# Two products of an encoder kernel by Strassen's algorithm for three of eight row pairs, with its sums on VectorE and in accumulating DMAs

## The chip, the cores and the metric

The kernel runs on one core of a Trainium2 chip. Its engines work beside one another, each through its own list of instructions in order: TensorE (PE, the matmuls, with their weight loads shown as PEld), VectorE (DVE), ScalarE (ACT), GpSimd (POOL), SyncE (SP, which here only issues DMAs), and the DMA engines. They wait for one another on semaphores. The metric is the device time of one launch in microseconds; the median of three runs before is 2689.91 us (2688.54 to 2690.1).

## What is computed

Two layers of an encoder over 256 tokens of width 2048, in float32, and a final norm:

```python
for l in range(DEPTH):                       # DEPTH = 2
    u = rmsnorm(x, norm_mix[l])
    proj = u @ w_in[l]
    ...                                      # latent attention y_a, neighbourhood attention y_b
    merged = jax.nn.sigmoid(gate_a) * y_a + jax.nn.sigmoid(gate_b) * y_b
    x = x + merged @ w_out[l]                # 2048 x 2048

    h = rmsnorm(x, norm_mlp[l]) @ w_ff1[l]   # 2048 x 8192
    x = x + jnp.square(jax.nn.relu(h)) @ w_ff2[l]   # 8192 x 2048

return rmsnorm(x, norm_final)
```

## The kernel before

x stays on the chip as two tiles `xt` of 128 tokens by 2048. All products run in a float32 made of two parts: an operand is split into `hi`, its value rounded to the matmul's type, and `lo`, the rest, and a product is the sum of three matmuls, hi x hi, hi x lo and lo x hi. An activation is kept transposed, 128 of its features by 256 tokens, as a tile `pair` whose left half is `hi` and right half `lo`. A weight is loaded once, as a 1 MB tile `raw` (L167, issued by SP, three buffers), cast to `hi` by ACT (L172) and subtracted to `lo` by DVE (L173), in pieces of 1024 columns with four buffers each (HBUFS).

There are two forms of product. `gemm_a` (L215) gives 128 tokens by 512 features: two PSUM banks, one for each half of the tokens, three matmuls of 512 columns for each 128 x 512 block of weight and half of the tokens (L199 to L201). `gemm_b` (L227) gives features by tokens: the weight is the stationary operand, and one matmul of 512 columns (both parts of the activation) and one of 256 (L194, L195) do a block. Of the eight PSUM banks five are for these products (`bank`) and three for attention, transposes and norms (`abank`).

A layer runs: w_in in pieces, with attention between them, gates and the two output projections, which merge into `part[t, c4]` (L597 to L600); w_out as four `gemm_a` of 512 features, whose sums are added to x by DVE (`residual`, L612, L617); then the MLP in four blocks of 2048 hidden features: `gemm_b` for w_ff1 (four calls of 512 features), squared ReLU (`relu2`, L639), `gemm_a` for w_ff2 (four calls), whose sums are multiplied by the squared norm scale and added to x by DVE (L619). The MLP's norm is thus applied after both products, as one factor for each token. In the last block, and after w_out, the squares of the new x are summed by ACT (L296) for the next norm, and the new x is transposed by PE (`turned_x`, L326) and split (L150, L154).

Engines get their instructions in the order in which a scheduler places them, and each executes its own in that order. Small work is written as generators that wait in `pending`: `tick`, called between the matmuls of a product, advances one that is due; `drain` runs all. So the transposes of the merged `part` for w_out stand between the matmuls of the next gate, those of x between the matmuls of the next product, and the norm's row (`rows_of`, L242, matmul L250) some 100 matmuls into the product after it.

## Time and profile before

| | |
|---|---|
| median of three runs | 2689.91 us |
| profiled execution: its time, its span | 2689.91 us, 2688.1 us |
| matmuls of `gemm_a` and attention's values, L199 to L201 | 3 x 2240 |
| matmuls of `gemm_b`, L194 and L195 | 2 x 3008 |
| weights loaded, with all other transfers | 496.49 MB, mean 185 GB/s |

The rows of the profile are read so. A group is the line of the program, the engine, the operation, the tile written and the tiles read, the sizes, the count; then the busy time of all in us, the mean of one in ns; then the idle time of the engine just ahead of them and what ended it. A row of a timeline is the start and length in us. The record of a matmul reaches past its slot, so the pace is read from the starts. In a row of a window the columns are the stretch, then for PE, PEld, DVE, ACT and POOL the busy us and the count, then PE's granted clock, the busy share of the DMA engines and GB/s. A wait is given as the waiting engine and line, what it waited for, the us in all, the times, the longest. A DMA group gives the queue, the count, the KB of each and the median us from issue to landing.

### The profile page before, as it was taken

To read this page: it belongs to the slowest core of one execution; us is meant where nothing else is said; L and a number is where in the kernel's file an instruction comes from. 1 tells how busy PE (TensorE), PEld (TensorE's weight loads), DVE (VectorE), ACT (ScalarE), POOL (GpSimd) and SP (SyncE) were. 2 spreads that over 40 slices of the span, in tenths; PEclk is the share of its full clock that TensorE was granted. 3 is DMA by queue.
4 is the path that set the end of the run, shared out by engine and by line. 5 is a ranking of instruction groups with operands and counts; after the bars stand their busy time and mean duration, and the time that the engine had idled before them with its cause. 6 is when DMAs were issued, how large, how long until landed. Compare 5 with 4: busy or idle time off the path is not lost.

```text
span 2688.1 us, 34037 instructions
## 1 busy us (share of the span) xinstructions
PE 2666.8 (99%) x13596; PEld 2268.7 (84%) x13596; DVE 1602.9 (60%) x2158; ACT 1277.1 (48%) x1815; POOL 60.5 (2%) x86
## 2 busy tenths in 40 slices
PE   8999999999999999999999999999999999999998
PEld 7888888888888888888888888888888888888886
DVE  5676486555655546556567754955556555565554
ACT  5554465444434434444445544644444344443443
POOL 1110000000000000000001100000000000000000
PEclk9999999999999999999999999999999999999999
DMA  7555644555565555555555555455555555655554
GB/s 231 184 165 189 195 161 155 189 184 180 186 203 186 190 190 186 197 193 189 183 183 179 171 187 183 153 167 188 188 188 188 189 187 194 208 189 193 188 188 141
DMA packets 253839, 496.49 MB, mean 185 GB/s; under 512 B 12688, under 2 KB 16784, under 8 KB 253680
## 3 DMA queue, kind: packets, MB, share of 16 engines
q1 hardware_dynamic: 250624, 488.14, 55.2%
q0 software_dynamic: 2048, 4.56, 0.6%
q8 instruction: 106, 1.74, 0.3%
q10 hardware_dynamic: 1008, 1.61, 0.2%
q14 instruction: 53, 0.43, 0.0%
HBM read 492.18 MB, written 2.10 MB: 184 GB/s over the span
## 4 chain that ended last, share of the span: by engine, by line
PE 84%; issue 14%; DVE 1%; DMA 1%; ACT 0%; POOL 0%; SPq 0%; POOLq 0%; DVEq 0%; ACTq 0%
PE bank L194 21%; PE bank L199 16%; PE bank L200 16%; PE bank L201 16%; PE bank L195 11%; DMA raw<-in_w_in 1%; PE abank L206 1%; PE abank L205 1%; PE abank L204 1%; PE abank L326 1%; PE abank L377 0%; DVE lo L173 0%; DVE wide L670 0%; PE abank L347 0%; ACT hi L172 0%
## 5 line engine op out<-in xcount | busy, mean ns | idle before, releaser
L173 DVE TENSOR_TENSOR lo<-raw,hi 128x1024 fp32r<-128x1024 f32 (+1 forms) x928 | 1132.5, 1222 | 977.8 <-ACT hi L172 973.0
L172 ACT CAST hi<-raw 128x1024 fp32r<-128x1024 f32 (+1 forms) x928 | 971.8, 1049 | 1131.1 <-PE bank L201 736.2
L194 PE MATMUL bank<-pair,hi 128*128 128x512 f32 x3008 | 1059.0, 398 | 2.3 <-DVE small L212 1.0
L200 PE MATMUL bank<-lo,pair 128*128 128x512 f32 (+1 forms) x2240 | 866.1, 387 | 0.0
L199 PE MATMUL bank<-hi,pair 128*128 128x512 f32 (+1 forms) x2240 | 865.8, 388 | 0.0
L201 PE MATMUL bank<-hi,pair 128*128 128x512 f32 (+1 forms) x2240 | 865.8, 387 | 0.0
L195 PE MATMUL bank<-pair,lo 128*128 128x256 f32 x3008 | 835.5, 280 | 0.4 <-DVE lo L173 0.3
L194 PEld LDWEIGHTS bank<-pair,hi 128*128 128x128 f32 x3008 | 563.5, 188 | 133.0 <-ACT hi L172 1.9
L195 PEld LDWEIGHTS bank<-pair,lo 128*128 128x128 f32 x3008 | 567.7, 189 | 5.9 <-DVE lo L173 1.6
L201 PEld LDWEIGHTS bank<-hi,pair 128*128 128x128 f32 x2240 | 420.8, 188 | 84.6
L199 PEld LDWEIGHTS bank<-hi,pair 128*128 128x128 f32 x2240 | 420.8, 188 | 84.1
L200 PEld LDWEIGHTS bank<-lo,pair 128*128 128x128 f32 x2240 | 420.9, 188 | 82.6
L150 ACT ACTIVATE pair<-small 128x256 fp32r<-128x256 f32 x200 | 73.6, 413 | 89.8 <-DVE small L641 67.1
L210 ACT COPY small<-bank 128x256 f32<-128x256 f32 x218 | 78.6, 369 | 29.0 <-PE bank L195 27.8
L152 DVE TENSOR_TENSOR pair<-small,pair 128x256 fp32r<-128x256 f32 x200 | 76.6, 418 | 19.2 <-ACT pair L150 19.2
L212 DVE TENSOR_TENSOR small<-bank,small 128x256 f32<-128x256 f32 x218 | 83.0, 416 | 0.2
L259 POOL TENSOR_TENSOR col<-var,mhalf 128x2 f32<-128x2 f32 x9 | 6.3, 702 | 1928.8 <-DVE var L257 1928.8
L619 DVE SCALAR_TENSOR_TENSOR xt<-bank,sq,xt 128x512 f32<-128x512 f32 x64 | 45.0, 744 | 7.8 <-PE bank L201 7.8
L641 DVE SCALAR_TENSOR_TENSOR small<-small 128x256 f32<-128x256 f32 x128 | 48.2, 418 | 0.0
L154 DVE SCALAR_TENSOR_TENSOR pair<-abank,g_sb,pair 128x256 fp32r<-128x256 f32 x64 | 29.2, 478 | 23.0 <-ACT pair L150 23.0
L150 ACT ACTIVATE pair<-abank,g_sb 128x256 fp32r<-128x256 f32 x64 | 28.2, 469 | 27.3 <-PE abank L326 23.4
L150 ACT ACTIVATE pair<-abank 128x256 fp32r<-128x256 f32 x64 | 23.6, 381 | 29.2 <-PE abank L206 19.1
(96 smaller groups left out, 789.9 us busy)
## 6 DMA issues: line engine op xcount, KB each, us to landing
raw<-in_w_ff SPq DMA_DIRECT2D x256, 1024.0 KB, 5.0
raw<-in_w_in SPq DMA_DIRECT2D x124, 1024.0 KB, 5.1
raw<-in_w_out SPq DMA_DIRECT2D x32, 1024.0 KB, 4.9
raw<-in_w_o_na SPq DMA_DIRECT2D x16, 1024.0 KB, 4.9
raw<-in_w_o_mla SPq DMA_DIRECT2D x16, 1024.0 KB, 4.9
raw<-in_w_ukv SPq DMA_DIRECT2D x8, 1024.0 KB, 4.9
raw<-in_w_uq SPq DMA_DIRECT2D x8, 768.0 KB, 4.6
raw<-in_w_in SPq DMA_DIRECT2D x10, 512.0 KB, 4.9
```

Source lines behind the costliest of these rows:

```text
L150: nc.scalar.activation(dst[:, :S], src, AF.Copy, scale=scale)
L152: nc.vector.tensor_tensor(dst[:, S:], src, dst[:, :S].bitcast(F32), op=ALU.subtract)
L172: nc.scalar.copy(hi, src)
L173: nc.vector.tensor_tensor(lo, src, hi.bitcast(F32), op=ALU.subtract)
L194: nc.tensor.matmul(ps, wh, a, start=first, stop=False)
L195: nc.tensor.matmul(ps[:, :S], wl, a[:, :S], start=False, stop=last)
L199: nc.tensor.matmul(ps, a[:, t * P:(t + 1) * P], wh, start=first, stop=False)
L200: nc.tensor.matmul(ps, a[:, t * P:(t + 1) * P], wl, start=False, stop=False)
L201: nc.tensor.matmul(ps, a[:, S + t * P:S + (t + 1) * P], wh, start=False, stop=last)
L210: nc.scalar.copy(h, ps[:, S:])
L212: nc.vector.tensor_tensor(t, ps[:, :S], h, op=ALU.add)
L641: nc.vector.scalar_tensor_tensor(t, t, 0.0, t, op0=ALU.max, op1=ALU.mult)
```

## The change

w_out and w_ff2 go to a new product, `gemm_s` (L360). It takes 256 rows of weight (a row pair j, eight in 2048 rows) by 1024 features as a 2 x 2 matrix of 128 x 512 blocks, and the activations for them as a 2 x 2 matrix of 128 features by 128 tokens. Five pairs are multiplied as before, 8 products of three matmuls each. The pairs in `SPAIRS`, 2, 4 and 6, are multiplied by Winograd's form of Strassen's algorithm, 7 products of three matmuls, for which four sums of weight blocks (`t`, L405 to L408) and four of activation blocks (`operand`, L333 to L336) are formed on DVE. All eight PSUM banks are in use: seven for the products, an eighth for the block that the ordinary pairs add to directly. One call covers 1024 features, so w_out is two calls (g = 0, 1), and w_ff2 two for each block. At its end `evac` adds the products up: a copy on ACT (L741), three sums on DVE (L742, L744, L746), then into x four products straight from PSUM on DVE (L748, L750 to L753) and four sums by `put`: on DVE (L735) in w_out and the last block, where squares of x follow, by accumulating DMAs from GpSimd (L733) in the first three blocks of each layer.

With it go other edits. `hi` and `lo` are 2048 columns wide in the second half of a layer, three buffers each; the pools of the two halves are opened and closed apart (`half_a`, `half_b`), and `drain` runs at the end of each. The transposes of `part` (`turned_pair`, L347) are started only after that drain, at the start of w_out. The MLP's norm is applied to the hidden features, as a row in `relu2` (L786), whose squares move to ACT (L787), so that the sums into x need no factor. The squares' sum of a Norm moves from GpSimd to DVE. The layer ends with a drain, which puts the next norm's row ahead of w_in's matmuls. The loads of the final gain move to the last block. One tag of eight PSUM banks takes the place of five and three.

```diff
-NSLOT, ABANKS, SMALL, RBUFS, HBUFS = 44, 3, 8, 3, 4
+NSLOT, SMALL, RBUFS, HBUFS = 44, 8, 3, 4
+SPAIRS = (2, 4, 6)
...
+            if hbufs == 3:
+                if k0 % 4 == 0:
+                    his = wpool.tile([P, 2048], F32R, tag="hi", name="hi", bufs=hbufs)
+                    los = wpool.tile([P, 2048], F32R, tag="lo", name="lo", bufs=hbufs)
...
-            nc.gpsimd.tensor_tensor(self.acc, self.acc, sq, op=ALU.add)
+            nc.vector.tensor_tensor(self.acc, self.acc, sq, op=ALU.add)
...
+    def operand(f, strassen):
+        a11, a21, a12, a22, s1, s2, s3, s4 = (f[:, i] for i in range(8))
+        if strassen:
+            nc.vector.tensor_tensor(s1, a21, a22, op=ALU.add)
+            nc.vector.tensor_tensor(s2, s1, a11, op=ALU.subtract)
+            nc.vector.tensor_tensor(s4, a12, s2, op=ALU.subtract)
+            nc.vector.tensor_tensor(s3, a21, a11, op=ALU.subtract)
+        hi, lo = [], []
+        for i in range(0, 8 if strassen else 4, 4):
+            src = f[:, i:i + 4].rearrange("p a q -> p (a q)")
+            h, lw = pair(), pair()
+            nc.scalar.copy(h, src)
+            nc.vector.tensor_tensor(lw, src, h.bitcast(F32), op=ALU.subtract)
...
+    def gemm_s(w, c0, acts, evac):
...
+        for j in range(n):
...
+            if j not in SPAIRS:
+                ws = parts(raw)
+                for k in range(2):
+                    left, right = ws[2 * k:2 * k + 2]
+                    ah, al = have(acts, j)
+                    for i, t, side in ((2, 0, right), (3, 0, left), (4, 1, right), (8, 1, left)):
+                        mm3(i, ah[2 * k + t], al[2 * k + t], *side)
...
+            b12, b11, b22, b21 = (raw[:, i:i + 512] for i in range(0, 2048, 512))
+            ts = wpool.tile([P, 4, 512], F32, tag="t", name="t", bufs=2)
+            t1, t3, t2, t4 = (ts[:, i] for i in range(4))
+            nc.vector.tensor_tensor(ts[:, :2], b12.rearrange("p (a n) -> p a n", a=1).to_broadcast([P, 2, 512]),
+                                    raw[:, 512:1536].rearrange("p (a n) -> p a n", a=2), op=ALU.subtract)
+            nc.vector.tensor_tensor(t2, b22, t1, op=ALU.subtract)
+            nc.vector.tensor_tensor(t4, b21, t2, op=ALU.subtract)
+            w11, w22, w21 = parts(raw[:, 512:])
+            w1, w3, w2, w4 = parts(ts.rearrange("p a n -> p (a n)"))
...
+            mm3(1, a11, l11, *w11)
+            mm3(2, a12, l12, *w21)
+            mm3(3, s4, r4, *w22)
+            mm3(5, s1, r1, *w1)
+            mm3(7, s3, r3, *w3)
+            mm3(6, s2, r2, *w2)
+            mm3(4, a22, l22, *w4)
+        evac(b)
...
-                if t == 1:
-                    start(turned(lambda t, c4=c4: part[t, c4], c4, mg, lambda c: 0.5), 2)
...
+        drain()
+        half_a.close()
...
+            def put(x, u):
+                if n is None:
+                    nc.gpsimd.dma_start(x, u, accum_op=ALU.add)
+                else:
+                    nc.vector.tensor_tensor(x, x, u, op=ALU.add)
...
+                nc.scalar.copy(p1, b[1])
+                nc.vector.tensor_tensor(u2, p1, b[6], op=ALU.add)
+                put(x11, p1)
+                nc.vector.tensor_tensor(u4, u2, b[5], op=ALU.add)
+                put(x12, u4)
+                nc.vector.tensor_tensor(u3, u2, b[7], op=ALU.add)
+                put(x21, u3)
+                nc.vector.tensor_tensor(x22, x22, b[5], op=ALU.add)
+                put(x22, u3)
+                nc.vector.tensor_tensor(x12, x12, b[3], op=ALU.add)
+                nc.vector.tensor_tensor(x11, x11, b[2], op=ALU.add)
+                nc.vector.tensor_tensor(x22, x22, b[8], op=ALU.add)
+                nc.vector.tensor_tensor(x21, x21, b[4], op=ALU.add)
...
-                nc.vector.scalar_tensor_tensor(t, t, 0.0, t, op0=ALU.max, op1=ALU.mult)
+                nc.vector.scalar_tensor_tensor(t, t, 0.0, mlp.row, op0=ALU.max, op1=ALU.mult)
+                nc.scalar.activation(relu2.f[:, 2 * (m % 2):2 * (m % 2) + 2].rearrange("p a q -> p (a q)"), t, AF.Square)
...
         if not last:
             start(norm.scales(), 10)
+            while pending:
+                drain()
+        half_b.close()
```

ACT at the first start of w_out, before: `th` is the gate's tanh, `hi` a weight, `pair` from `abank` the transposed and scaled `part`.

```order
L533 ACTIVATE th<-bank,half 128x512 x2
L172 CAST hi<-raw 128x1024 x7
L150 ACTIVATE pair<-abank 128x256 x3
L172 CAST hi<-raw 128x1024
L150 ACTIVATE pair<-abank 128x256
L172 CAST hi<-raw 128x1024 x5
```

The same place in the changed program; `f` is the transposed `part`, L382 the weights of `gemm_s`.

```order
L643 ACTIVATE th<-bank,half 128x512 x2
L189 CAST hi<-raw 128x1024
L355 ACTIVATE f<-bank 128x512
L341 CAST pair<-f 128x512
L382 CAST hi<-raw 128x2048 x2
L355 ACTIVATE f<-bank 128x512
L341 CAST pair<-f 128x512
L355 ACTIVATE f<-bank 128x512
L382 CAST hi<-raw 128x1536
```

Before, casts of weights went on between the copies of the transposed tiles, with several casts ahead of each; now the first copy and its cast stand ahead of the first weight of w_out.

DVE in the first block of w_ff2 before, where one call follows another: `lo` is a weight's rest, `xt_91` and `xt_92` the two tiles of x.

```order
L173 TENSOR_TENSOR lo<-raw,hi 128x1024 x7
L619 SCALAR_TENSOR_TENSOR xt_91<-bank,sq,xt_91 128x512
L619 SCALAR_TENSOR_TENSOR xt_92<-bank,sq,xt_92 128x512
L173 TENSOR_TENSOR lo<-raw,hi 128x1024 x8
L619 SCALAR_TENSOR_TENSOR xt_91<-bank,sq,xt_91 128x512
```

The same in the changed program, where its second call follows the first: `wide` is a sum of the evacuation, `xt_88` and `xt_89` are x, `t` the sums of weights.

```order
L742 TENSOR_TENSOR wide<-wide,bank 128x512
L383 TENSOR_TENSOR lo<-raw,hi 128x2048
L744 TENSOR_TENSOR wide<-wide,bank 128x512
L746 TENSOR_TENSOR wide<-wide,bank 128x512
L748 TENSOR_TENSOR xt_89<-xt_89,bank 128x512
L383 TENSOR_TENSOR lo<-raw,hi 128x2048
L751 TENSOR_TENSOR xt_88<-xt_88,bank 128x512
L405 TENSOR_TENSOR t<-raw 128x1024
L383 TENSOR_TENSOR lo<-raw,hi 128x1536
L750 TENSOR_TENSOR xt_88<-xt_88,bank 128x512
L753 TENSOR_TENSOR xt_89<-xt_89,bank 128x512
L407 TENSOR_TENSOR t<-raw,t 128x512
```

Two updates of x between runs of equal `lo` have become eight steps that stand between the next call's `lo` and its sums of weights.

PE where the second layer begins, before: L194 and L195 are w_in's matmuls, L250 the norm's row.

```order
L194 MATMUL bank<-pair,hi 128x512
L195 MATMUL bank<-pair,lo 128x256
L250 MATMUL abank<-diag,ones 128x128 x2
L194 MATMUL bank<-pair,hi 128x512
L195 MATMUL bank<-pair,lo 128x256
```

The changed program: L432 are the transposes of x, L267 the norm's row, L211 and L212 w_in's matmuls.

```order
L377 MATMUL bank<-hi,pair 128x512
L432 MATMUL bank<-ident,xt_88 128x128 x4
...
L432 MATMUL bank<-ident,xt_89 128x128
L267 MATMUL bank<-diag,ones 128x128
L211 MATMUL bank<-pair,hi 128x512 x4
L267 MATMUL bank<-diag,ones 128x128
L212 MATMUL bank<-pair,lo 128x256
L211 MATMUL bank<-pair,hi 128x512
```

The row's matmuls have moved from within w_in's stream to its head.

## The prediction

> **What bounds the kernel now.** I read the page's busy shares first, then the windows, then what PE waited for.

> ```profile
> span 2688.1 us, 34037 instructions
> PE 2666.8 (99%) x13596; PEld 2268.7 (84%) x13596; DVE 1602.9 (60%) x2158; ACT 1277.1 (48%) x1815; POOL 60.5 (2%) x86
> PE 84%; issue 14%; DVE 1%; DMA 1%; ACT 0%; POOL 0%; SPq 0%; POOLq 0%; DVEq 0%; ACTq 0%
> 700.00:800.00 100.00, 100.00 (x480) 84.04 (x480) 56.33 (x67) 43.55 (x53) 0.00 (x0) 1.00 0.58 192
> PE abank L326 <- DMA xt<-in_x: 7.4, 3, 4.5
> PE bank L194 <- ACT hi L172: 1.0, 2, 0.7
> ```

> PE is busy 2666.8 of 2688.1 us and busy for the whole of a stretch inside the second MLP product (700 to 800 us). Its longest wait, 7.4 us in three pieces, is for the first rows of x. So TensorE bounds every stage: a matmul taken away is worth its slot, and whatever makes PE wait costs in full, since no other wait stands in its shadow. The execution profiled took 2689.91 us, 1.8 outside its span, which is also the median of the three runs; the sum is made against it.

> The slot, and the pace of the engines that feed PE, come from a timeline in that product:

> ```profile
> 745.04 0.39 PE L199 MATMUL bank<-hi,pair 128*128 128x512 f32 x1
> 745.24 1.05 ACT L172 CAST hi<-raw 128x1024 fp32r<-128x1024 f32 x1 [1.67 <-PE bank L201]
> 745.27 0.39 PE L200 MATMUL bank<-lo,pair 128*128 128x512 f32 x1
> 746.33 1.23 DVE L173 TENSOR_TENSOR lo<-raw,hi 128x1024 fp32r<-128x1024 f32 x1 [1.50 <-ACT hi L172]
> 747.96 1.05 ACT L172 CAST hi<-raw 128x1024 fp32r<-128x1024 f32 x1 [1.67 <-PE bank L201]
> 750.19 1.40 DVE L619 SCALAR_TENSOR_TENSOR xt<-bank,sq,xt 128x512 f32<-128x512 f32 x2
> ```

> Between two casts lie 2.72 us and 12 matmuls: 0.2267 us each. A cast starts some 0.2 us after the matmul that freed its tile ended its slot, and `lo` 0.04 after `hi`. Two dependent 0.744 us operations of DVE take 1.40 together, so its pitch is about 0.09 under the recorded length.

> ```profile
> L173 DVE TENSOR_TENSOR lo<-raw,hi 128x1024 fp32r<-128x1024 f32 x912 | 1117.4, 1226 | 972.5 <-ACT hi L172 967.7 <-PE bank L195 1.0
> L188 DVE TENSOR_TENSOR lo<-raw,hi 128x512 fp32r<-128x512 f32 x8 | 5.2, 689 | 5.3 <-ACT hi L187 5.3
> L172 ACT CAST hi<-raw 128x1024 fp32r<-128x1024 f32 x912 | 958.6, 1052 | 1123.9 <-PE bank L201 730.3 <-PE bank L194 363.2 <-issue 12.4
> L187 ACT CAST hi<-raw 128x512 fp32r<-128x512 f32 x8 | 4.6, 618 | 7.8 <-PE bank L194 7.8
> L617 DVE TENSOR_TENSOR xt<-xt,bank 128x512 f32<-128x512 f32 x16 | 10.2, 681 | 0.0
> L173 DVE TENSOR_TENSOR lo<-raw,hi 128x768 fp32r<-128x768 f32 x16 | 15.1, 954 | 5.3 <-ACT hi L172 5.3
> L246 DVE TENSOR_SCALAR diag<-ident,col 128x128 f32<-128x128 f32 x12 | 2.9, 281 | 1.6 <-POOL col L259 1.6
> L296 ACT ACTIVATE junk<-xt 128x512 f32<-128x512 f32 x40 | 25.2, 630 | 13.4 <-DVE xt L619 9.9 <-DMA xt<-in_x 2.9
> L296 ACT ACTIVATION_READ_ACCUMULATOR junk<-xt 128x1 f32 x40 | 7.5, 188 | 0.0
> L154 DVE SCALAR_TENSOR_TENSOR pair<-abank,g_sb,pair 128x256 fp32r<-128x256 f32 x64 | 29.2, 478 | 23.0 <-ACT pair L150 23.0
> L308 DVE TENSOR_SCALAR half<-col 128x2 f32<-128x2 f32 x2 | 1.1, 572 | 1.2 <-POOL col L259 1.2
> ```

> 512 more columns cost DVE 0.54 us and ACT 0.43. Carried on, a 2048-wide `lo` has 2.31 (pitch 2.23), a 1536-wide one 1.77 (1.68), a 2048-wide `hi` 1.92. Pitches of the others: 0.60 for 512, 1.14 for 1024, 0.2 for 128 (estimates from these rows). A square with its read-out holds ACT for some 0.74.

> **What goes.** Twenty calls of the new product (two layers, ten GEMMs of 1024 columns by two) have three pairs each with 21 matmuls for 24: 180 fewer, 180 x 0.2267 = **40.8 us**, 2.04 a call. Transposes stay in number.

> **What DVE gets.** A call holds PE for 183 x 0.2267 = 41.5 us. In it DVE has five 2048-wide `lo` (11.2), three times the weight sums and two `lo` of a Strassen pair (1.14 + 2 x 0.60 + 1.68 + 2.23, 18.8) and eight steps of the evacuation (4.8): 34.8. Where the four sums into x are also DVE's (w_out and the last block), 37.2. In w_out the operands of the first call add eleven `lo` and twelve 128-wide sums: 9.0. So the mean fits beneath PE everywhere, but order decides at the joints. In a Strassen stretch the three hi/lo buffers turn in 0.2 + 1.92 + 0.04 + 2.31 + 0.08 = 4.55 us against 21 matmuls, 4.76: hidden, by 0.2, and in addition by the `hi` matmuls that can go ahead of `lo`.

> **What PE waits for.** I followed each joint with these pitches; PE's waits:

> - Start of w_out, 3.5 x 2 layers = 7.0. Four transposes (0.45) are PE's last work; then ACT has the copy `f` (about 0.62), the cast to `pair` (0.62) and only then a 2048-wide `hi` (1.92), with handoffs of 0.2 at both ends: 3.95. Before, the transposes stood inside a running stream and nothing waited.
> - First w_out call, 1.8 x 2 = 3.6. From the first `hi` DVE needs 15.1 us to the `lo` of the first Strassen sums (three 2048-wide `lo`, 6.7; one of 1536, 1.7; two rounds of weight sums, 4.7; two operand `lo` and four operand sums, 2.0); PE has 48 + 9 matmuls and 20 transposes to do until then, 15.1 too. At the three tiles after it operand sums go on standing ahead of `lo`, and PE is held 0.2, 0.2 and 0.8; 0.6 for a dozen dependent steps of DVE, 0.05 each.
> - w_out, first to second call, 2.8 x 2 = 5.6. Counted from PE's start of the second call, DVE ends its second `lo` at 1.8, and has 7.6 (seven steps of 512, 4.8 with the x sums; a 1024-wide sum; a 1536-wide `lo`) to the last update of x, 9.4. ACT's squares wait for that, three of them end at 11.6; behind them the `hi` of the sums ends at 13.6, the next tile's at 15.5 and its `lo` at 18.1. PE has 54 matmuls and 16 transposes, 14.0, and is held 1.3 for that `hi` and 1.2 for that `lo`, with handoffs 2.8.
> - First product of the MLP, 3.0 x 2 = 6.0. PE has eight chunks of x, each four pairs of a 512- and a 256-column matmul (0.35, a little over one and a half slots): 11.2, and 16 transposes: 13.0. The squares end at 10.7; mean square, power (0.71, below), `half` (0.57) and diagonals (0.2 each) with their handoffs stand on DVE until 13.2, then a 2048-wide `lo` until 15.6, then the split of the ninth chunk (0.48), 16.1.
> - Last block, first to second call: 2.8 x 2 = 5.6, as in w_out.
> - Boundary of the layers, 4.3. The last update ends 1.4 after PE, four squares then end at 4.4, and mean square, power, diagonal and three handoffs take 1.7; the matmul for the row now stands ahead of w_in's stream, so PE waits 6.1 less its 16 transposes (16 x 0.11).
> - End: 1.6, for two updates and three queued squares after PE's last matmul, where one update and one square stood.
> - The other twelve calls, one handoff of 0.2 each, 2.4; the rows of the MLP norm, 0.5; seven further handoffs, 1.4.

> The end of the kernel before, the power that it and the boundary share, and from the chain of waits six transposes (0.11 us each):

> ```profile
> 2676.53 0.39 PE L201 MATMUL bank<-hi,pair 128*128 128x512 f32 x1
> 2676.96 0.75 DVE L619 SCALAR_TENSOR_TENSOR xt<-bank,sq,xt 128x512 f32<-128x512 f32 x1 [0.61 <-PE bank L201]
> 2677.80 0.63 ACT L296 ACTIVATE junk<-xt 128x512 f32<-128x512 f32 x1 [0.63 <-DVE xt L619]
> 2679.01 0.71 POOL L259 TENSOR_TENSOR col<-var,mhalf 128x2 f32<-128x2 f32 x1 [365.60 <-DVE var L257]
> 457.76 0.66 PE abank L326 x6
> ```

> Sum of the waits 38.0, so the change comes to 38.0 - 40.8 = -2.8 us: 2687.1, say **2687**. The terms that hang on order (3.6, 5.6, 6.0, 5.6: 20.8) are the soft ones: at a third of that the time is 2673, at half as much again 2697.

> **Accumulating DMAs.** 12 calls issue four each, 256 KB, from tile to tile. The trace has no such transfer; the nearest:

> ```profile
> out<-wide SPq DMA_DIRECT2D x8, 256.0 KB, 2.1
> mb<-in_rpb POOLq DMA_DIRECT2D x32, 96.0 KB, 3.2
> wide<-in_gain_fin POOLq DMA_DIRECT2D x4, 256.0 KB, 5.2
> xt<-in_x ACTq DMA_DIRECT2D x6, 256.0 KB, 9.3
> ```

> So 2.1 to 9.3 us. DVE meets x12 again 6.9 us after its sum was issued (between them stand L746, L748, a `lo`, L751, L405 and a 1536-wide `lo`: 0.6 + 0.6 + 2.23 + 0.6 + 1.14 + 1.68), x21 after as long, and behind a late x on DVE stand the weight sums L407 and L408 and the next `lo`, for which PE waits. I take 5.2, the row of the same queue and size: hidden. That `lo` is some 1.5 us early, so PE feels a landing past about 8.3 us, at the six first-to-second joints; after a second call the next product leaves some 10 us. Were DVE to do these sums itself it would be charged 2.4 us a call. Their 12.6 MB are hidden beneath a mean DMA share of 0.58 (the window above). The norm's sum that moves from GpSimd to DVE is hidden by DVE's idle share.

> **The clock after a pause.** The kernel's start has the only pauses:

> ```profile
> 9.80 1.81 PE L326 MATMUL abank<-ident,xt 128*128 128x128 f32 x7 [1.03 <-DMA xt<-in_x]
> 14.40 0.63 PE L194 MATMUL bank<-pair,hi 128*128 128x512 f32 x1
> 15.26 0.63 PE L194 MATMUL bank<-pair,hi 128*128 128x512 f32 x1
> 20.25 0.40 PE L194 MATMUL bank<-pair,hi 128*128 128x512 f32 x1
> 20.62 0.40 PE L194 MATMUL bank<-pair,hi 128*128 128x512 f32 x1
> ```

> At 14 to 17 us a 512-column and two 256-column matmuls take 0.86 us; at 20 us a pair takes 0.37. That is half the pace, from 12.3 to past 17, and costs 2.5 us or more after waits that sum to 7.4 us with only transposes between. [...]

> **Rivals.** (1) Waits mostly hidden: instructions overlap more than my joints allow, as DVE's idle 40% permits. The 20.8 falls to a third: 2673. For it: in the trace PE's queue goes on with `hi` matmuls when `lo` is late; against it: DVE and ACT issue in order, and the long pieces stand in one line. (2) Slower by late sums: a landing of 10 to 12 us, since four transfers share engines that loads hold for half the time. From 8.3 us on, DVE's stall passes to PE: 3 us a joint and the ramp behind it lost, at six joints 18 to 24: 2708. The 9.3 row speaks for it, the 5.2 row against. (3) Half rate after each of three pauses: 3 x 2.5 = 7.5: 2695. (4) The ring is the bound in every call: were a 2048-wide `lo` and `hi` 0.4 us longer together than carried on from 512 and 1024, a turn takes 4.95 for 4.76, and the six tiles that follow one another in a call's Strassen stretch lose 0.19 each, 1.1 us a call, 23 in twenty: 2710. For it speaks that no 2048-wide operation is in the trace, against it that the rows of 512, 768 and 1024 lie on one line. (5) The matmuls are not saved: the row below has 3 x 2240 = 6720 on its three lines, and the changed program lists 6540 on the lines that take their place, so this is left 0.01.

> ```profile
> L199 PE MATMUL bank<-hi,pair 128*128 128x512 f32 (+1 forms) x2240 | 865.8, 388 | 0.0
> ```

> **Chances.** Forecast 0.37, rival 1 0.27, rival 2 0.13, rival 3 0.15, rival 4 0.07, the last 0.01. 0.2%, about what a measurement of this kernel can tell from no change, is 5.4 us: 2684.5 to 2695.3. Rival 1 and 0.10 of the forecast give faster, 0.37; 0.24 of the forecast and 0.08 of rival 3 same, 0.32; the rest slower, 0.31. Both signs hold much, so: the forecast's own range is 2679 to 2697; to hold 8 in 10 it reaches from 2667 (the soft terms nearly gone) to 2712 (rivals 2 and 4).

> **What would show it.** PE's busy time down by 40 us with the span nearly as before: the rest must be PE's waits, named `hi` L382 (start of w_out), `lo` L383 (joints) and the diagonal L267 (boundary). If the twelve clean calls run in 41.5 us, the ring is right. A late DMA shows as DVE's L750 or L752 waiting for POOL's queue; half rate as spacings of 0.43 us after a pause. I am wrong if PE's waits come to 25 us or less, or if the twelve calls of blocks 0 to 2 hold more than 6 us of them.

## The result and the profile after

| | before | after |
|---|---|---|
| median | 2689.94 us (beside the runs of after) | 2733.14 us (2730.55 to 2734.91) |
| ratio of after to before | | 1.0161, 95% interval 1.0143 to 1.0179 |
| span of the profiled execution | 2688.1 us | 2730.1 us |

The changed kernel is 1.6% slower, above the upper end of the predicted range. The page of after:

```profile
span 2730.1 us, 33460 instructions
PE 2665.4 (98%) x13424; PEld 2244.4 (82%) x13424; DVE 1911.6 (70%) x2310; ACT 1377.9 (50%) x1701; POOL 94.5 (3%) x122
PE 56%; issue 31%; DVE 6%; DMA 3%; ACT 2%; POOL 1%; POOLq 0%; DVEq 0%; ACTq 0%
L382 ACT CAST hi<-t 128x2048 fp32r<-128x2048 f32 x60 | 114.7, 1911 | 122.2 <-PE bank L377 63.3
L383 DVE TENSOR_TENSOR lo<-t,hi 128x2048 fp32r<-128x2048 f32 x60 | 137.4, 2290 | 15.1 <-ACT hi L382 14.8
xt<-wide POOLq DMA_DIRECT2D x48, 256.0 KB, 6.8
```

PE executes 172 instructions fewer, yet its busy time is down by 1.4 us and not by 40: those that are left take longer, in their pace or at half clock (both below). The new 2048-wide operations take what was carried on for them, 1.91 us on ACT and 2.29 on DVE. What PE waited for, in all, times and the longest:

```profile
PE bank L377 <- ACT hi L382: 13.0, 13, 3.1
PE bank L377 <- DVE lo L383: 11.7, 15, 1.3
PE bank L211 <- DVE pair L162: 6.9, 4, 2.9
PE bank L267 <- DVE diag L263: 4.8, 1, 4.8
PE bank L211 <- ACT hi L189: 4.8, 1, 4.8
```

With four further rows, that of x's first load the longest (6.0), the list sums to 50.6 us, against 10.0 before. The last row shown, x's first load and 1.2 of the 6.9 us for `pair` are the kernel's start, 12.0 us in all, where before has 9.0; the first matmul of w_in starts at 12.1 us in one and at 12.3 in the other. Behind the start 38.6 us are left, against 1.0 before. So 37.6 us of waits are new; the forecast has 36.4 for PE (38.0 with 1.6 at the end). They have the names foretold, but for 3.2 us in attention (two further rows, L221 and L453), which no term names. The saving of 40.8 should have paid for all this: for a span that is 42.0 us longer two more causes are needed, and both stand in windows. First, a stretch of 95 us within the gates and output projections, code that the change doesn't touch, before and then after. After the length come PE's busy time and its count:

```profile
250.00:345.00 95.00, 95.00 (x420) 78.68 (x420) 46.21 (x41) 40.49 (x41) 0.00 (x0) 1.00 0.58 186
```

```profile
250.00:345.00 95.00, 95.00 (x416) 78.02 (x415) 45.68 (x41) 40.14 (x41) 0.00 (x0) 1.00 0.60 191
```

In both PE never rests and the granted clock is 1.00, but after gets through 416 matmuls where before did 420. The mean from start to start over the whole trace went from 227.0 to 229.0 ns for the 6540 matmuls that move a weight; for the 3008 pairs of `gemm_b`, which move `pair`, from 350.4 to 353.1 ns. That is 13.1 + 8.1 = **21.2 us** everywhere in the program. Second, four windows in which the clock (the number ahead of the last two) was granted by half:

```profile
553.00:559.50 6.50, 5.99 (x22) 5.32 (x23) 6.01 (x4) 5.65 (x7) 0.00 (x0) 0.50 0.34 109
669.00:672.30 3.30, 3.29 (x10) 2.81 (x11) 1.75 (x4) 2.14 (x6) 0.00 (x0) 0.50 0.78 228
1375.60:1378.90 3.30, 3.19 (x10) 2.81 (x11) 3.14 (x6) 2.08 (x3) 0.00 (x0) 0.50 0.00 0
1911.50:1914.80 3.30, 3.30 (x11) 2.72 (x12) 3.30 (x2) 2.48 (x3) 0.00 (x0) 0.50 0.01 1
```

In the clock's own record these are 6.83, 3.41, 3.41 and 3.41 us, 17.1 in all, of which half is lost: **8.5 us** (an estimate: half of the time at half clock). Each follows a pause of PE (3.13, 2.86, 4.80 and 3.13 us). The first, at w_out's start, in PE's timeline without the weight loads:

```profile
553.51 1.65 PE L377 MATMUL bank<-hi,pair 128*128 128x512 f32 x3 [3.13 <-ACT hi L382]
554.95 1.06 PE L352 MATMUL bank<-ident,wide 128*128 128x128 f32 x4
555.66 0.78 PE L377 MATMUL bank<-hi,pair 128*128 128x512 f32 x1
...
560.15 0.40 PE L377 MATMUL bank<-lo,pair 128*128 128x512 f32 x1
560.39 0.39 PE L377 MATMUL bank<-hi,pair 128*128 128x512 f32 x1
```

After a pause of 3.13 us a matmul is recorded with 0.78 us; at 560.39, 0.23 after its forerunner, with 0.39.

The first matmuls of each stage, from both timelines, give where the span grew, in us (the last two columns belong to two experiments below; a stage ends where the next one's first matmul starts, the last block with its last matmul):

| stage | after | weights at 256 | the same without Strassen |
|---|---|---|---|
| up to w_out in the first layer | +6.4 | +3.1 | +2.7 |
| w_out, both layers | +16.0 | +12.9 | +6.2 |
| first w_ff1, both | +11.2 | +6.9 | +0.9 |
| w_ff2 of blocks 0 to 2 with the w_ff1 behind it, six | -7.1 | -10.6 | +4.6 |
| w_ff2 of the last block, both | -0.6 | -1.3 | -0.8 |
| end of the first layer to the second w_out | +13.8 | +11.1 | +12.0 |
| end | +2.3 | +2.4 | +1.4 |
| in all | +41.9 | +24.4 | +27.1 |

### The profile page after: what moved, and what is told of

It is laid out like the page before. It is cut to its first block, busy times and chain, and to the rows that moved or that the text cites. A ratio compares the mean times of both kernels' runs of the same rounds, so it can differ in the third digit from the quotient of the medians.

```text
span 2730.1 us, 33460 instructions
## 1 busy us (share of the span) xinstructions
PE 2665.4 (98%) x13424; PEld 2244.4 (82%) x13424; DVE 1911.6 (70%) x2310; ACT 1377.9 (50%) x1701; POOL 94.5 (3%) x122
## 4 chain that ended last, share of the span: by engine, by line
PE 56%; issue 31%; DVE 6%; DMA 3%; ACT 2%; POOL 1%; POOLq 0%; DVEq 0%; ACTq 0%
PE bank L211 15%; PE bank L216 8%; PE bank L218 8%; PE bank L217 8%; PE bank L212 7%; PE bank L377 7%; DVE lo L383 3%; POOL xt L733 1%; DMA xt<-wide 1%; ACT hi L382 1%; DMA raw<-in_w_ff 1%; DMA raw<-in_w_out 1%; PE bank L221 1%; PE bank L223 1%; PE bank L222 1%
## 5 line engine op out<-in xcount | busy, mean ns | idle before, releaser
L211 PE MATMUL bank<-pair,hi 128*128 128x512 f32 x3008 | 1073.0, 400 | 11.7 <-DVE pair L162 6.9
L212 PE MATMUL bank<-pair,lo 128*128 128x256 f32 x3008 | 843.0, 282 | 0.0
L377 PE MATMUL bank<-hi,pair 128*128 128x512 f32 x2440 | 767.6, 394 | 13.0 <-ACT hi L382 13.0
L211 PEld LDWEIGHTS bank<-pair,hi 128*128 128x128 f32 x3008 | 567.6, 189 | 147.0 <-DVE pair L162 8.0
L190 DVE TENSOR_TENSOR lo<-raw,hi 128x1024 fp32r<-128x1024 f32 (+1 forms) x352 | 426.5, 1214 | 351.7 <-ACT hi L189 350.9
L189 ACT CAST hi<-raw 128x1024 fp32r<-128x1024 f32 (+1 forms) x352 | 364.3, 1041 | 414.7 <-PE bank L218 309.0
L212 PEld LDWEIGHTS bank<-pair,lo 128*128 128x128 f32 x3008 | 566.3, 188 | 2.2
L377 PEld LDWEIGHTS bank<-hi,pair 128*128 128x128 f32 x2440 | 458.5, 189 | 116.5 <-ACT hi L382 19.6
L377 PE MATMUL bank<-lo,pair 128*128 128x512 f32 x1220 | 481.5, 395 | 12.2 <-DVE lo L383 11.7
L182 DVE TENSOR_TENSOR lo<-raw,hi 128x2048 fp32r<-128x2048 f32 x128 | 293.2, 2291 | 201.9 <-ACT hi L181 201.9
L383 DVE TENSOR_TENSOR lo<-raw,hi 128x2048 fp32r<-128x2048 f32 (+1 forms) x160 | 331.3, 2088 | 110.5 <-ACT hi L382 110.5
L382 ACT CAST hi<-raw 128x2048 fp32r<-128x2048 f32 (+1 forms) x160 | 277.5, 1750 | 256.2 <-PE bank L377 200.6
L181 ACT CAST hi<-raw 128x2048 fp32r<-128x2048 f32 x128 | 244.4, 1910 | 265.5 <-PE bank L211 225.4
L216 PE MATMUL bank<-hi,pair 128*128 128x512 f32 (+1 forms) x960 | 370.8, 387 | 0.0
L218 PE MATMUL bank<-hi,pair 128*128 128x512 f32 (+1 forms) x960 | 369.8, 386 | 0.0
L217 PE MATMUL bank<-lo,pair 128*128 128x512 f32 (+1 forms) x960 | 367.0, 382 | 0.0
L217 PEld LDWEIGHTS bank<-lo,pair 128*128 128x128 f32 x960 | 180.4, 188 | 36.4
L382 ACT CAST hi<-t 128x2048 fp32r<-128x2048 f32 x60 | 114.7, 1911 | 122.2 <-PE bank L377 63.3
L383 DVE TENSOR_TENSOR lo<-t,hi 128x2048 fp32r<-128x2048 f32 x60 | 137.4, 2290 | 15.1 <-ACT hi L382 14.8
## 6 DMA issues: line engine op xcount, KB each, us to landing
xt<-wide POOLq DMA_DIRECT2D x48, 256.0 KB, 6.8
```

Of the source, the lines that this page charges most:

```text
L181: nc.scalar.copy(his, raw)
L182: nc.vector.tensor_tensor(los, raw, his.bitcast(F32), op=ALU.subtract)
L189: nc.scalar.copy(hi, src)
L190: nc.vector.tensor_tensor(lo, src, hi.bitcast(F32), op=ALU.subtract)
L211: nc.tensor.matmul(ps, wh, a, start=first, stop=False)
L212: nc.tensor.matmul(ps[:, :S], wl, a[:, :S], start=False, stop=last)
```

## The experiments

**What sets the pace.** In the built program of the kernel before, `raw`, `hi` and `lo` start at multiples of 256 bytes in each partition, and so does `pair`. The changed one has a new pool, `keep` (8512 bytes, with the norm's rows and diagonals), ahead of the weights' pools, and these start 64 bytes past a multiple, `pair` at one; its scratch for DMAs is 8192 bytes in place of 16384. Six kernels move tiles and nothing else.

Of after, with an unused tile of 64 bytes, so that the weights start at 128:

```diff
     keep = ctx.enter_context(tc.tile_pool(name="keep", bufs=2))
+    keep.tile([P, 16], F32, tag="pad", name="pad", bufs=1)
```

> The changed kernel with an unused 64-byte tile ahead of its weight pools, so that hi and lo start at a multiple of 128 bytes, as they did in the kernel before, and not 64 past one. In the changed kernel every matmul with a weight starts 2.0 to 2.2 ns later than before (226.7 to 228.9 ns for 512 columns, 116.8 to 118.2 for 256), in code that the diff leaves alone too. Theory A, the start address of hi and lo: the pace is again 226.7 and about 116.5 ns, and 12,556 such matmuls give back 25 to 27 us: 2706 us (2703 to 2711). Rival B, something else that the change brings everywhere (eight banks in one rotation, the smaller scratch, weights in another region): pace and time as in the changed kernel, 2733 us.

It got slower, which neither theory had: 2739.32 us, ratio 1.0190 [1.0173, 1.0207]. The window of 95 us has 411 matmuls:

```profile
250.00:345.00 95.00, 95.00 (x411) 77.03 (x410) 45.25 (x40) 39.01 (x40) 0.00 (x0) 1.00 0.60 189
```

A multiple of 128 is no cure, then; but that the start matters at all is shown. The kernel before with its tiles shifted, weights to 64 and `pair` to 128 (the smaller scratch makes room for the two tiles):

```diff
+    slots.tile([P, 16], F32, tag="pad", name="pad", bufs=1)
...
+    const.tile([P, 16], F32, name="pad")
...
-    nc = bacc.Bacc("TRN2", target_bir_lowering=False, num_devices=1)
+    nc = bacc.Bacc("TRN2", target_bir_lowering=False, num_devices=1, dynamic_dma_scratch_size=8192)
```

> The kernel before with the scratch of 8192 bytes as in the changed kernel and 64 bytes put ahead of its weight pool alone (the slots of the activations stay at multiples of 128), nothing else. Theory A: 12,736 matmuls with a weight each 2.0 to 2.2 ns slower, pace 228.9 and 118.2 ns, 2717 us (2713 to 2720). Rival B: 2690 us.

2731.65 us, 1.0157 [1.0142, 1.0173]: the kernel before, with not one instruction changed, loses 42 us by its tiles' places alone, and more than theory A's 2717. That it comes out beside after is chance: its matmuls that move a weight take 233.3 ns, those of after 229.0.

```profile
250.00:345.00 95.00, 95.00 (x409) 76.14 (x408) 45.26 (x40) 38.62 (x40) 0.00 (x0) 1.00 0.59 188
```

The smaller scratch by itself:

> The kernel before with the scratch of 8192 bytes of the changed kernel and nothing else; every tile moves by 8192 bytes, so starts stay multiples of 256. Theory A2: pace 226.7 ns and 2689.5 us (2687 to 2692). Rival B3, the smaller scratch is what slowed the shifted kernel: 2715 to 2732 us.

2689.27 us, 1.0001 [0.9992, 1.0011]: nothing. After with 192 bytes in place of 64, so that the weights start at a multiple of 256 as before:

> The changed kernel with 192 unused bytes ahead of its weight pools. The runs so far, by the start of hi and lo and of pair past a multiple of 256 bytes: 0 and 0, 226.7 ns for 512 columns; 64 and 0, 228.9; 128 and 0, 232.4; 64 and 128, 233.3. Theory A2, each matmul is slower by how far its operands start past a multiple of 256: with 0 and 0 the pace is 226.7 and about 116.8 ns again, and the time 2733 less 25 to 27: 2707 us (2703 to 2711). Rival B2, the pace is a lottery of each program that has no tie to these addresses: some other pace between 226 and 234, time 2700 to 2745.

2719.97 us (2714.47 to 2721.31), 1.0112 [1.0097, 1.0127]: the pace of the matmuls that move a weight came as theory A2 says, the time did not (2703 to 2711). The window:

```profile
250.00:345.00 95.00, 95.00 (x421) 78.69 (x420) 46.49 (x42) 40.46 (x41) 0.00 (x0) 1.00 0.58 186
```

13.2 us less than after by medians, 17.4 by spans (its profiled execution had 6.8 us of half clock, that of after 17.1). By the mean of `gemm_b`'s pairs, 351.8 ns, some 4 of the 21.2 us remained. Two readings were left: that each operand's start has its price, or that the distance between the two has. The scratch kernel with `pair` at 128 and the weights at 0, then with both at 64:

```diff
+    slots.tile([P, 32], F32, tag="pad", name="pad", bufs=1)
```

```diff
     xt = [const.tile([P, D], F32, name=f"xt{t}") for t in range(2)]
+    const.tile([P, 16], F32, name="pad")
```

> The kernel before with the small scratch (which alone changed nothing) and its activations, pair, moved 128 bytes past a multiple of 256; hi and lo stay at a multiple. Theory A2 in its additive form (64 on hi costs 2.2 ns a matmul that moves a weight, 128 on pair the rest of the 6.3): 231.2 ns for such a matmul, 2689 + 28 = 2717 us (2712 to 2722). Rival G (only the operand that moves counts, the address of pair only in the product where pair moves): 227 ns, 2689 to 2695 us.

> The kernel before with an unused tile of 64 bytes ahead of the weight pools, so that weights (raw, hi, lo) and activations (pair) both start 64 bytes past a multiple of 256; in the kernel before both start at a multiple. No instruction differs. Theory A (the pace of a matmul that moves a weight follows the difference of the two starts, modulo 256, whatever each start is): the difference is 0 again, start to start 227.0 ns, time within 0.1% of before, 2687 to 2692. Theory B (each start costs by itself, and the costs add): 229 ns for the weights' 64 and half of what 128 did for pair (232.6 - 227.0, so 2.8), 231 to 232 ns in all, 2705 to 2730.

2727.06 us, 1.0140 [1.0124, 1.0156], outside both ranges, and 2688.55 us, 0.9997 [0.9988, 1.0006], as its theory A has it. Their windows, in that order:

```profile
250.00:345.00 95.00, 95.00 (x409) 76.43 (x408) 45.21 (x40) 38.66 (x40) 0.00 (x0) 1.00 0.58 187
```

```profile
250.00:345.00 95.00, 95.00 (x421) 78.67 (x420) 46.21 (x41) 40.29 (x42) 0.00 (x0) 1.00 0.58 188
```

With both at 64 nothing is lost; it is the distance that costs (weights' start less that of `pair`; in `gemm_b`, where `pair` moves, the other way round, in brackets):

| start of weights, of `pair`, modulo 256 | distance | start to start, a weight moves, ns | pair of `gemm_b`, ns |
|---|---|---|---|
| 0, 0 (before) and 64, 64 | 0 | 227.0, 227.0 | 350.4, 350.1 (0) |
| 0, 0 (after with 192 bytes) | 0 | 227.1 | 351.8 (0) |
| 64, 0 (after) | 64 | 229.0 | 353.1 (192) |
| 128, 0 and 0, 128 | 128 | 232.4, 232.6 | 351.0, 350.9 (128) |
| 64, 128 | 192 | 233.3 | 350.9 (64) |

Why it does is not shown. The pairs of `gemm_b` follow it less, and not it alone: at the same distance of 0 they take 350.4 ns in before and 351.8 in the changed kernel with 192 bytes. That is open.

**What Strassen's algorithm is worth.** The restructured kernel with `SPAIRS = ()`, so that all pairs are multiplied by eight products and the first four steps and the four sums of `evac` fall away, in the layout of 128 and in that of 256:

> As the aligned changed kernel, but with no pair by Strassen: 24 matmuls for 21, no sums of weights or activations, and four updates of x on DVE straight from PSUM. Theory A (what is lost beside the address lies at joints where DVE's sums, evacuation steps and squares stand in line, and in three pauses that the order of the layer makes): the 40.8 us of matmuls come back, the waits at the joints go (some 25 us), the pauses at the start of w_out, at the first MLP product and at the boundary stay with their half-rate phases: 2715 us (2705 to 2725). Rival C (the waits come from the wider tiles and the order, not from Strassen's steps): the aligned kernel plus 41, 2747 us.

> As the changed kernel with the 192 bytes, but no pair by Strassen (24 matmuls for 21, no sums of weights or activations, four updates of x straight from PSUM). Theory A2 on the pace; the run with 64 bytes and no Strassen took 12 us more than its partner, so the net of Strassen was 12 and not 41, with 29 of waits: 2707 + 12 = 2719 us (2713 to 2726). Rival C: nothing of the waits is Strassen's, 2707 + 41 = 2748 us.

2751.31 us (2749.57 to 2752.45), 12.0 above its twin with Strassen; and 2717.79 us (2717.01 to 2719.0), 2.2 below its own, though by spans 2.5 above. The first lies above both theories, the second in its range by luck: its twin was taken to be at 2707 and 12 us below it. So in the layout without the address's cost the 40.8 us saved are given back within the executions' scatter, and the other edits together cost 28.8 us. The table's last two columns say where: without Strassen w_out and the first w_ff1 are 12.7 us shorter and blocks 0 to 2 are 15.2 longer, although twelve calls save 24.5; the other 9.3 go at their joints. Why Strassen keeps 12.0 us in the layout of 128 and nothing here is not shown. The pauses in the last column (+6.2 in w_out, +12.0 at the boundary) have nothing to do with Strassen, since there is none.

w_out by the old `gemm_a`, its transposes again between the gate's matmuls, no drain ahead; in the layout of 128 and in that of 256:

```diff
-        drain()
         half_a.close()
...
-        for g in range(2):
-            gemm_s(w_out[l], g * 1024, mg, ...)
+        for c4 in range(4):
+            gemm_a(w_out[l], c4 * 512, mg, plain(c4))
```

> As the aligned changed kernel, but w_out by the old product of 512 features, its operand's transposes back between the gates' matmuls, two updates of x for each call. The profile of the changed kernel loses 8.1, 5.2 and 4.2 us over the two calls of w_out and the first MLP product in layer 0 and 7.5, 5.2 and 3.0 in layer 1 (half-rate phases among it). Theory A: most of these 33 us go, some 8.2 of matmuls come back, 3 to 6 at the first MLP product stay: 2685 us (2681 to 2692). Rival D (the waits are of the half's end and merely move into w_out's old calls): 2700 us or more.

> As the changed kernel with the 192 bytes, but w_out by the old product of 512 features, its transposes back between the gates' matmuls. Theory A2 on the pace; the run with 64 bytes and this product took 13 us less than its partner: 2707 - 13 = 2694 us (2688 to 2700). Rival B2: pace and time free, 2690 to 2735.

2726.13 us, 13.2 less than its twin, and 2701.41 us, 1.0045 [1.0030, 1.0060], 18.6 less; both lie above theory A's ranges, the first with the slow pace of its layout. So the new form of w_out, with its drain and its late transposes (the three were not taken apart), costs 18.6 us more than the 8.2 us that its 36 matmuls save. The second run also has some of the shortest pauses that were followed by the half clock (second layer, start of w_out):

```profile
1891.14 0.99 PE L433 MATMUL bank<-ident,wide 128*128 128x128 f32 x7 [0.94 <-DVE wide L711]
1893.35 0.80 PE L218 MATMUL bank<-lo,pair 128*128 128x512 f32 x1 [1.22 <-DVE lo L183]
1893.94 0.63 PE L219 MATMUL bank<-hi,pair 128*128 128x512 f32 x1
...
1896.80 0.39 PE L218 MATMUL bank<-lo,pair 128*128 128x512 f32 x1
```

Two waits of 0.94 and 1.22 us with seven transposes between; the same place in the first layer, with the same two waits, kept its clock. The traces show what differs. In each of the seventeen the clock changes only at points of a grid of 3.413 us (to 5 ns). It fell 34 times ahead of the kernels' ends, each time behind a stretch of that grid in which PE, transposes counted as work, was idle for 58% or more; no stretch at full clock with 56% or less was followed by a fall, and none lay between. In after the four falls stand behind stretches in which PE worked for 0.89, 0.62, 0.00 and 0.35 of 3.41 us (from 549.48, 665.53, 1372.09 and 1907.99 us on), and the idlest one behind which the clock stayed has 1.90 (from 1334.55). The stretches at the two starts of w_out:

```profile
548.37:551.79 3.42, 2.32 (x14) 1.57 (x12) 3.35 (x5) 2.35 (x3) 0.00 (x0) 1.00 0.00 0
1889.79:1893.20 3.41, 1.40 (x10) 0.89 (x8) 3.38 (x3) 2.35 (x3) 0.00 (x0) 1.00 0.02 5
```

PE works for 2.32 us of the first and for 1.40 of the second: the grid cuts the same two waits in the one layer and holds nearly all of both in the other. So where a pause falls on the grid decided here, as well as its length.

**The accumulating DMAs.** DVE waits for them in after, in all, times and the longest:

```profile
DVE xt L752 <- DMA xt<-wide: 19.0, 12, 2.1
```

The layout of 256 with all sums into x on DVE:

```diff
-                if n is None:
-                    nc.gpsimd.dma_start(x, u, accum_op=ALU.add)
-                else:
-                    nc.vector.tensor_tensor(x, x, u, op=ALU.add)
+                nc.vector.tensor_tensor(x, x, u, op=ALU.add)
```

> The changed kernel with 192 bytes, all sums into x on DVE, no accumulating DMA. The DMAs landed in 6.8 us (median) where 5.2 was taken; DVE's last two updates waited for them 19 us in twelve calls in the changed kernel. Theory A (they are hidden, nearly): DVE has 2.4 us more in each of twelve calls, it has 4.2 to spare in the mean, but the joint gets later: 0 to 1.5 us more at six joints, 2720 to 2729. Rival F (late landings are what PE waits for at the clean joints): 5 to 10 us less, 2710 to 2715.

2720.46 us (2717.63 to 2722.47) beside 2719.97: no difference. Their landing, 6.8 us, makes DVE wait and PE not.

**A version that beats both was sought and not found.** w_out by `gemm_a` within the first half's pools, no drain at the layer's end:

> The kernel with 192 bytes and the old w_out, and three edits more: w_out still in the first half's pools (1024-wide hi and lo, four buffers), no drain at the end of a layer, and the pool of small tiles ahead of the slots, so that pair and hi start at the same place past a multiple of 1024. Theory A: the pauses at the start of w_out go (in its partner 2.7 and 4.2 us, a half-rate phase among it), of the 7.4 at the boundary some 6 go, a pair of matmuls with the weight held takes 350.4 ns for 351.8 (4 us): 2701 - 17 = 2684 us (2679 to 2690), the first that beats the kernel before. Rival E: the pauses only move, to the first MLP product and to w_in, where the pools change hands: 2695 us or more.

2704.81 us (2700.75 to 2709.1), as rival E has it; and the pairs of `gemm_b` took 352.8 ns, not 350.4. The pauses went on to the next changes of pools:

```profile
PE bank L212 <- ACT hi L190: 9.8, 2, 4.9
PE bank L212 <- ACT hi L182: 6.8, 2, 3.4
```

(Half of the first row is the kernel's start.) Then with the second half's tiles laid out in another order, and with that and no Strassen:

```diff
+            turn_lo = wpool.tile([P, 1024], F32R, tag="lo", name="lo", bufs=hbufs)
+            nc.gpsimd.memset(turn_lo[:, :1].bitcast(F32), 0.0)
...
-        wpool = half_b.enter_context(tc.tile_pool(name="wpool2", bufs=4, reuse_waits="tile"))
-        tmp = half_b.enter_context(tc.tile_pool(name="tmp2", bufs=2, reuse_waits="tile"))
+        wpool = tmp = half_b.enter_context(tc.tile_pool(name="wpool2", bufs=4, reuse_waits="tile"))
+        tmp.tile([P, 8, P], F32, tag="f", name="f", bufs=2)
+        small()
+        wpool.tile([P, 2048], F32, tag="raw", name="raw", bufs=RBUFS)
+        wpool.tile([P, 4, 512], F32, tag="t", name="t", bufs=2)
```

> The kernel with the old w_out, w_ff2 by Strassen's algorithm, no drain at the layers' ends and weights at a multiple of 256 (2704.81 us), changed in the order alone in which tiles lie in the second half's pool, so that the first hi, lo and raw of each half take room that was free before the last matmul of the half ahead; two one-column memsets on GpSimd in each layer turn the ring of lo by two. Theory A (the new pools' tiles standing on the room of the old make the pauses of 3.4 and 4.9 us at the two changes, and the pauses bring on the half clock): the waits for hi and lo at the first product of the MLP and at the second layer's w_in fall from 16.6 us to below 6, the half clock from 17 us to below 4, the time to 2678 to 2690. Theory B (the pauses are the loads' or the norm row's): the time stays at 2698 to 2708, with other names on the waits.

> The kernel of the run before with no pair by Strassen's algorithm (SPAIRS empty; the first four steps of its sums at a call's end fall away). Sixteen calls lose 9 matmuls saved each: 144 x 0.227 = 32.7 us more of matmuls. Theory A (with the joints' waits at about 1 to 1.5 us a call, Strassen's algorithm pays in w_ff2): slower than the run before by 10 to 20 us. Theory B (what it saves goes wholly into the joints, as with the layout of the change): within 4 us of the run before.

2704.37 us (2700.89 to 2707.22): theory A is refuted, the waits are the same to 0.3 us.

```profile
PE bank L212 <- ACT hi L190: 9.5, 2, 4.9
PE bank L212 <- ACT hi L182: 6.8, 2, 3.4
```

Without Strassen 2716.27 us (2714.7 to 2719.09), 11.9 more: here, in w_ff2 alone, Strassen keeps 11.9 of the 32.7 us that its 144 matmuls hold. Last, the pools changed two weight tiles into the next product, which puts casts ahead of the last squares of x on ACT:

> The run with moved rings (2704.37 us), changed at the two changes of pools alone: the pools are changed only behind the first two weight tiles of the next product, which still come from the old ones. ACT's list then has casts of the next product ahead of the last squares of x (at the start of the MLP two or three, at the second layer's start one of 2048 columns), where the run before had the first cast behind them. Theory A (the pauses of 3.4, 3.4 and 4.9 us come of that order on ACT, and the half clock of the pauses): the waits for hi at these three places fall from 11.7 us to below 4, the half clock from 10 us or more to below 4, the time to 2682 to 2692. Theory B (the loads or the norm's row come late whatever the order): 2698 to 2708, with the waits under other names.

2705.19 us (2700.69 to 2707.64):

```profile
PE bank L212 <- ACT hi L190: 9.1, 2, 5.6
PE bank L212 <- ACT hi L182: 4.5, 2, 2.3
PE bank L213 <- DVE lo L183: 2.3, 2, 1.1
```

At the start of the MLP the wait was split and not shortened (2.3 for `hi` and 1.1 for `lo`, where 3.4 for `hi` stood); at the boundary it fell from 4.9 to 3.5. The half clock has 6.8 us for 13.7 in the profiled executions, of which this run's was its fastest, and the median stayed. Theory A is refuted: at the start of the MLP the order on ACT only changes what PE waits for, and at the boundary it is at most a part of the cause. What makes these pauses, and the 15 us that are left to the kernel before, is open.

## Why the prediction was wrong

By spans the forecast was 2688.1 - 2.8, and 2730.1 came: 44.8 us over. They are pace 21.2, half clock 8.5, and 15.1 of joints: 42.0 + 40.8 - 21.2 - 8.5 leaves 53.1 of waits and short steps, where 38.0 were forecast. The list of waits has only 37.6 of the 53.1. From start to start the same pauses are some 46 us longer than before, since a matmul's record reaches 0.16 us past its slot (0.39 for 0.23) and a wait is counted from its end. The kernel's end has 2.3, and the last 5 or so lie in steps too short for the list.

- **The step that failed** is the one taken as a matter of course: the durations of the trace before were carried over to all that the change leaves alone, 0.2267 us a slot. It was true of the layout, not of the instruction. The change moves tiles, and 9548 slots, or pairs of them, became 2.0 or 2.7 ns longer. The shifted kernel before shows this cause by itself, at a distance of 192, and the layout of 256 takes most of it away from the changed one. No rival had it. Between 0 and 192 bytes of distance lie 42 us (2731.65 for 2689.43).
- **The matmuls saved** were rightly counted: 6540 weight-moving matmuls are left of 6720, 40.8 us. The last rival is out.
- **Half rate after pauses** was seen at the kernel's start and has no term in the sum. The third rival had 7.5 us for three pauses, at the two starts of w_out and at the boundary, by the 2.5 us of the kernel's start; that each of them would be followed by half rate was the author's estimate, and before, with 1.0 us of waits behind its start, has no such pause after dense work to show it. 8.5 came, in four phases, two of them after the pauses at w_out's start, one at the first MLP product and one at the boundary; so this term was put at nothing, and the rival had it nearly right. Each phase is one or two times 3.41 us long (6.83 and three of 3.41), and a stretch of that length idle by 58% was enough.
- **The single pauses** came nearly as worked out: 3.1 us for 3.5 at w_out's start (the pieces named there, 0.62 + 0.62 + 1.92 and two handoffs of 0.2, sum to 3.56 and not to 3.95, which gives the 3.1), 2.9 for 3.0 at the first MLP product, 4.8 + 0.2 for 4.3 at the boundary, 1.34 + 0.36 for 1.8 in w_out's first call (2.5 from start to start), 2.3 for 1.6 at the end.
- **The joints of second calls** were taken too small. In the last block of the first layer:

```profile
1334.97 0.96 PE L377 MATMUL bank<-hi,pair 128*128 128x512 f32 x3 [0.84 <-ACT hi L382]
1337.71 0.50 PE L377 MATMUL bank<-lo,pair 128*128 128x512 f32 x1 [1.09 <-DVE lo L383]
1346.00 0.97 PE L377 MATMUL bank<-hi,pair 128*128 128x512 f32 x3 [0.67 <-ACT hi L382]
1349.81 0.50 PE L377 MATMUL bank<-lo,pair 128*128 128x512 f32 x1 [1.13 <-DVE lo L383]
```

  The first two waits are those of the prediction, 1.9 for 2.5. The second pair, 11 us later at the next Strassen pair, was not worked out. That DVE had not caught up, since by the prediction a Strassen stretch has 0.2 us a turn to spare, is argued and not tested. With short steps behind each, 5.2 us for 2.8 there and in w_out's second calls; in the last block of the second layer 1.7 for 2.8.
- **Twelve clean calls** were given 0.2 us each. The six first calls hold that: they run in 41.9 us, which is 183 x 0.2289, and in 41.5 at the pace of 227.0, as foretold. The six second ones lose 0.9 to 2.0 us each from start to start, 7.9 in all, where 2.4 were given to all twelve. That is over the 6 us named as the sign of error, though the waits in the profile are only 3.4 of it; the sign for the waits, 25 us or less, was not met. With the second calls above and the 2.2 us more in attention this is most of the 15.1.
- **Late sums** (rival 2) and **the ring** (rival 4) are out: DVE's L752 did wait for the DMAs (19.0 us), the sign named for rival 2, but with the sums on DVE the time is the same (2720.46 us for 2719.97); and the wide operations have the durations carried on (1.91 and 2.29 us for 1.92 and 2.31).

## What to carry to other kernels

A diff that adds a pool ahead of others moves tiles, and moved tiles changed the pace of matmuls that nobody touched, here from 227.0 ns to 229.0 in after and to 233.3 in the shifted kernel before; so compare PE's count in one full window of unchanged code before and after, ahead of any talk of waits. A saving on the engine that bounds is worth what is left after its joints: here, with DVE at 70%, 40.8 us of matmuls became 2 lost to 12 kept. A pause of PE cost its length and, where it left 58% or more of a stretch of the 3.413 us grid idle, half of 3.41 or 6.83 us more from the clock (the half is an estimate).
